# DoRA forward on Trainium2: hand-made semaphores in one critical section, and TensorE's blocks as a loop inside one instruction page

## The chip, the cores and the metric

The kernel runs on one core of a Trainium2 chip. The metric is the device time in microseconds (us) of one execution, the median of ten. Beside it stands one profiled execution: its span runs from the first to the last instruction of the program, and a little more time lies around it.

## The reference

```python
W_adapted = W + scale * (lora_A @ lora_B)
W_norm = np.sqrt(np.sum(W_adapted ** 2, axis=0, keepdims=True) + 1e-8)
W_final = W_adapted / W_norm * m
y = x.reshape(-1, 256) @ W_final          # x: 16 x 2048 x 256, float32
```

W is 256 x 256, the rank is 16. x and y are 33.5 MB each, so 67.1 MB cross between HBM and the on-chip memory.

## The kernel before

The 32,768 rows of x are cut into 8 blocks of 4,096 rows (`BLK`), 4 MB each; a partition holds 32 rows of a block. Five buffers hold x blocks (`XBUFS = 5`), and y is written over x in the same buffer. A block is worked in 8 chunks of 4 rows per partition (`CH`, 64 chunks in all, `NCH`).

Setup: three small loads are issued by ScalarE (lora_A, lora_B, m), W by SyncE, and then SyncE issues the loads of blocks 0 to 4. Meanwhile the engines compute `w_final` (bfloat16) from W, lora_A, lora_B and m in a chain that alternates between TensorE, VectorE (DVE) and ScalarE (ACT); its last step is the multiplication of line 132.

Each chunk goes through four engines. GpSimd (POOL) rounds x to bfloat16 (`xb`, L148). TensorE transposes it in four instructions, two bfloat16 values read as one float32 (`xt_ps`, L151). DVE copies the result to on-chip memory (`xt`, L155). TensorE multiplies it with `w_final` in 8 matmuls (`y_ps`, L166). ACT copies y into the x buffer (L174). TensorE's order is written out by hand: the transposes of chunk g+1 stand before the multiplies of chunk g, but at the end of a block the multiplies come first. Everything on TensorE is unrolled: 64 chunks one after the other.

After the last chunk of a block SyncE issues its store (L178), and, from block 1 on, the load of block b+4 into the buffer of block b-1 (L62), which waits until the store of block b-1 has landed. All loads and stores of x and y go through SyncE's queue (q1), the three small loads through ACT's (q10). Semaphores and waits are placed by the tile framework. In the profile the queues of kind "instruction" (q8 and q14) carry the engines' own program.

Of the kernel before, what the change touches and what calls it, by code (L numbers as in the profile page):

```python
# [10 lines left out]
@with_exitstack  # L11
def kernel(
    ctx: ExitStack,
    tc: tile.TileContext,
    x: bass.AP,
    W: bass.AP,
    lora_A: bass.AP,
    lora_B: bass.AP,
    m: bass.AP,
    scale: float,  # L20
    out: bass.AP,
):
    nc = tc.nc
    P = 128
    FP32 = mybir.dt.float32
    BF16 = mybir.dt.bfloat16
    AF = mybir.ActivationFunctionType
    ALU = mybir.AluOpType

    x_flat = x.flatten_outer_dims()  # L30
    out_flat = out.flatten_outer_dims()
    N, IN = x_flat.shape
    OUT = W.shape[1]
    R = lora_A.shape[1]
    KC = IN // P
    J = 4
    DJ = 32
    BLK = DJ * P
    NBLK = N // BLK

    assert IN == OUT and IN % P == 0 and OUT % P == 0 and N % BLK == 0

    XBUFS = 5
    CH = DJ // J
    NCH = NBLK * CH

    consts = ctx.enter_context(tc.tile_pool(name="consts", bufs=1))
    startup = ctx.enter_context(tc.tile_pool(name="startup", bufs=1))
    xpool = ctx.enter_context(tc.tile_pool(name="xpool", bufs=XBUFS))
    xbpool = ctx.enter_context(tc.tile_pool(name="xbpool", bufs=3))  # L50
    xtpool = ctx.enter_context(tc.tile_pool(name="xtpool", bufs=3))
    pp_xt = ctx.enter_context(tc.tile_pool(name="pp_xt", bufs=4, space=bass.MemoryType.PSUM))
    pp_y = ctx.enter_context(tc.tile_pool(name="pp_y", bufs=2, space=bass.MemoryType.PSUM))


    ctx.enter_context(tc.manual_schedule())

    x_tiles = {}

    def load_x(b):  # L60
        t = xpool.tile([P, DJ, IN], FP32, name="x_sb", tag="x_sb")
        nc.sync.dma_start(  # L62
            out=t,
            in_=x_flat[b * BLK : (b + 1) * BLK].rearrange("(p j) k -> p j k", p=P),
        )
        x_tiles[b] = t


    a_nat = startup.tile([P, KC, R], FP32)
    nc.scalar.dma_start(out=a_nat, in_=lora_A.rearrange("(p t) r -> p t r", t=KC))  # L70
    w_nat = startup.tile([P, KC, OUT], FP32)
    nc.sync.dma_start(out=w_nat, in_=W.rearrange("(p t) o -> p t o", t=KC))
    b_nat = startup.tile([R, OUT], FP32)
    nc.scalar.dma_start(out=b_nat, in_=lora_B)
    m_row = startup.tile([1, OUT], FP32)
    nc.scalar.dma_start(out=m_row, in_=m[None, :])
    for b in range(XBUFS):
        load_x(b)

    identity = consts.tile([P, P], FP32)  # L80
    make_identity(nc, identity)
    ones = consts.tile([P, P], FP32)
    nc.vector.memset(ones, 1.0)
    eps_col = startup.tile([P, 1], FP32)
    nc.vector.memset(eps_col, 1e-8)

    warm = startup.tile([P, 1], FP32)
    nc.scalar.activation(out=warm, in_=eps_col, func=AF.Sqrt)  # L88


    w_final = consts.tile([P, KC, OUT], BF16)

    b_bf = startup.tile([R, OUT], BF16)
    nc.vector.tensor_copy(out=b_bf, in_=b_nat)  # L94

    aT_ps = pp_y.tile([R, KC * P], FP32, tag="psy", name="aT_ps")
    for t in range(KC):
        nc.tensor.transpose(aT_ps[:, t * P : (t + 1) * P], a_nat[:, t, :], identity)  # L98
    aT = startup.tile([R, KC * P], BF16)
    nc.vector.tensor_copy(out=aT, in_=aT_ps)  # L100

    ab_ps = pp_y.tile([P, KC, OUT], FP32, tag="psy", name="ab_ps")
    for t in range(KC):
        nc.tensor.matmul(  # L104
            ab_ps[:, t, :], aT[:, t * P : (t + 1) * P], b_bf, start=True, stop=True
        )

    wa = startup.tile([P, KC, OUT], FP32)
    nc.vector.scalar_tensor_tensor(  # L109
        out=wa, in0=ab_ps, scalar=float(scale), in1=w_nat, op0=ALU.mult, op1=ALU.add  # L110
    )
    sq = startup.tile([P, KC, OUT], FP32)
    nc.vector.tensor_mul(out=sq, in0=wa, in1=wa)  # L113


    n2_ps = pp_y.tile([P, OUT], FP32, tag="psy", name="n2_ps")
    for t in range(KC):
        nc.tensor.matmul(n2_ps, ones, sq[:, t, :], start=(t == 0), stop=(t == KC - 1))  # L118
    norm = startup.tile([P, OUT], FP32)
    nc.scalar.activation(out=norm, in_=n2_ps, func=AF.Sqrt, bias=eps_col)  # L120

    mb_ps = pp_y.tile([P, OUT], FP32, tag="psy", name="mb_ps")
    nc.tensor.matmul(mb_ps, ones[0:1, :], m_row, start=True, stop=True)  # L123
    m_all = startup.tile([P, OUT], FP32)
    nc.vector.tensor_copy(out=m_all, in_=mb_ps)  # L125
    wam = startup.tile([P, KC, OUT], FP32)
    for t in range(KC):
        nc.vector.tensor_mul(out=wam[:, t], in0=wa[:, t], in1=m_all)  # L128
    rnorm = startup.tile([P, OUT], FP32)
    nc.vector.reciprocal(out=rnorm, in_=norm)  # L130
    for t in range(KC):
        nc.vector.tensor_mul(out=w_final[:, t], in0=wam[:, t], in1=rnorm)  # L132

    j_order = []
    for a in range(J // 2):
        j_order.append(a)
        j_order.append(a + J // 2)


    xts = {}  # L140

    def transposed(g):
        b, c = divmod(g, CH)
        rows = x_tiles[b][:, c * J : (c + 1) * J, :]


        xb = xbpool.tile([P, J, IN], BF16, name="xb")
        nc.gpsimd.tensor_copy(out=xb, in_=rows)  # L148
        xt_ps = pp_xt.tile([P, J * P], FP32, tag="psxt", name="xt_ps")
        for j in range(J):  # L150
            nc.tensor.transpose(  # L151
                xt_ps[:, j * P : (j + 1) * P], xb[:, j, :].bitcast(FP32), identity
            )
        xt = xtpool.tile([P, J * P, KC], BF16, name="xt")
        nc.vector.tensor_copy(  # L155
            out=xt.rearrange("p r t -> p (r t)").bitcast(FP32), in_=xt_ps
        )
        xts[g] = xt

    def multiplied(g):  # L160
        b, c = divmod(g, CH)
        xt = xts.pop(g)
        y_ps = pp_y.tile([P, J, OUT], FP32, tag="psy", name="y_ps")
        for t in range(KC):
            for j in j_order:
                nc.tensor.matmul(  # L166
                    y_ps[:, j, :],
                    xt[:, j * P : (j + 1) * P, t],
                    w_final[:, t, :],
                    start=(t == 0 and (j % (J // 2)) == 0),  # L170
                    stop=(t == KC - 1 and (j % (J // 2)) == (J // 2) - 1),
                )

        nc.scalar.copy(out=x_tiles[b][:, c * J : (c + 1) * J, :], in_=y_ps)  # L174


        if c == CH - 1:
            nc.sync.dma_start(  # L178
                out=out_flat[b * BLK : (b + 1) * BLK].rearrange("(p j) k -> p j k", p=P),
                in_=x_tiles[b],  # L180
            )
            if b >= 1 and b - 1 + XBUFS < NBLK:
                load_x(b - 1 + XBUFS)

    transposed(0)
    for g in range(NCH):


        first = (g + 1) % CH == 0
        if first:  # L190
            multiplied(g)
        if g + 1 < NCH:
            transposed(g + 1)
        if not first:
            multiplied(g)


# [33 lines left out]
```

## Time and profile before

| what | value |
|---|---|
| median of ten runs | 165.51 us (165.28 to 165.94) |
| the profiled execution, its own time | 165.39 us |
| its span | 163.5 us |
| bytes read from and written to HBM | 33.85 and 33.55 MB, 412 GB/s over the span |
| share of the span of q1, the queue of x and y | 96.6% of 16 DMA engines |
| ACT, POOL busy | 66.4 us, 66.5 us |
| TensorE matmul busy | 100.8 us |
| median from issue to landing: load of x, store of y | 29.3 us, 34.0 us |

The page cuts the span into 40 slices and gives for each the busy share in tenths. The chain of waits follows the work that ended last back to its beginning. In the queue table, the columns are packets, MB and share of 16 engines' span. In tables by stretch of time each row has the length of the stretch, the busy time (and count) of PE, its weight loads, DVE, ACT and POOL, TensorE's granted clock, the DMA share and GB/s. Single packets of the DMA queues, with start, length and size, are in the trace as well; times are counted from the span's start. A load or store of one block is 128 packets of 32,768 bytes, 8 on each of the 16 DMA engines, and leaves one packet of 4 bytes on each engine when that engine's share is done.

These waits of SyncE's queue show when SyncE stands still (us in total, times, longest):

```profile
SPq L178 <- ACT x_sb L174: 63.7, 5, 17.6
SPq L62 <- DMA out_dram<-x_sb: 49.1, 3, 22.1
SPq L226 <- DMA out_dram<-x_sb: 23.2, 1, 23.2
```

### The profile page before, as it was taken

To read this page: it belongs to the slowest core of one execution; us is meant where nothing else is said; L and a number is where in the kernel's file an instruction comes from. 1 tells how busy PE (TensorE), PEld (TensorE's weight loads), DVE (VectorE), ACT (ScalarE), POOL (GpSimd) and SP (SyncE) were. 2 spreads that over 40 slices of the span, in tenths; PEclk is the share of its full clock that TensorE was granted. 3 is DMA by queue.
4 is the path that set the end of the run, shared out by engine and by line. 5 is a ranking of instruction groups with operands and counts; after the bars stand their busy time and mean duration, and the time that the engine had idled before them with its cause. 6 is when DMAs were issued, how large, how long until landed. Compare 5 with 4: busy or idle time off the path is not lost.

```text
span 163.5 us, 2035 instructions
## 1 busy us (share of the span) xinstructions
PE 100.8 (62%) x778; PEld 84.9 (52%) x778; DVE 50.5 (31%) x76; ACT 66.4 (41%) x67; POOL 66.5 (41%) x70
## 2 busy tenths in 40 slices
PE   0264799999999999992009993299704997000000
PEld 0042589798898797991007891289603895000000
DVE  0228535455453654450003450055301352000000
ACT  3010147677678677674000675027800378000000
POOL 1005757687685886810029510595007750000000
PEclk9999999999999999999555899579995799955555
DMA  5998998999999999999999999999999999999981
GB/s 196 461 441 385 497 401 385 485 409 425 457 397 369 401 477 399 425 449 405 465 417 417 457 425 409 465 409 437 441 417 425 457 417 421 433 433 441 433 385 56
DMA packets 2635, 67.53 MB, mean 413 GB/s; under 512 B 433, under 2 KB 450, under 8 KB 578
## 3 DMA queue, kind: packets, MB, share of 16 engines
q1 hardware_dynamic: 2448, 67.37, 96.6%
q8 instruction: 6, 0.10, 0.2%
q10 hardware_dynamic: 178, 0.03, 0.1%
q14 instruction: 3, 0.02, 0.0%
HBM read 33.85 MB, written 33.55 MB: 412 GB/s over the span
## 4 chain that ended last, share of the span: by engine, by line
DMA 59%; PE 17%; DVE 4%; ACT 2%; issue 1%; POOL 1%; ACTq 0%; SPq 0%; POOLq 0%
DMA out_dram<-x_sb 38%; DMA x_sb<-in_x_dram 18%; PE y_ps L166 9%; PE xt_ps L151 5%; DMA b_nat<-in_lora_B_dram 3%; ACT x_sb L174 2%; PE n_ps L118 1%; DVE w_final L132 1%; DVE rnorm L130 1%; PE mb_ps L123 1%; POOL xb L148 1%; DVE wam L128 0%; DVE sq L113 0%; DVE wa L109 0%; PE ab_ps L104 0%
## 5 line engine op out<-in xcount | busy, mean ns | idle before, releaser
L148 POOL CAST xb<-x_sb 128x1024 bf16<-128x1024 f32 x64 | 65.8, 1046 | 66.1 <-DMA x_sb<-in_x_dram 47.1
L174 ACT COPY x_sb<-y_ps 128x1024 f32<-128x1024 f32 x64 | 64.4, 1013 | 62.4 <-PE y_ps L166 37.8
L166 PE MATMUL y_ps<-w_final,xt 128*128 128x256 bf16 x512 | 70.7, 286 | 2.3 <-DVE xt L155 2.3
L155 DVE COPY xt<-xt_ps 128x512 f32<-128x512 f32 x64 | 43.8, 691 | 75.6 <-PE xt_ps L151 75.6
L151 PE MATMUL xt_ps<-identity,xb 128*128 128x128 f32 x256 | 43.0, 301 | 26.4 <-POOL xb L148 26.4
L166 PEld LDWEIGHTS <-xt 128*128 128x128 bf16 x512 | 51.1, 102 | 12.7 <-DVE xt L155 5.8
L151 PEld LDWEIGHTS xt_ps<-identity,xb 128*128 128x128 f32 x256 | 33.4, 156 | 29.9 <-POOL xb L148 29.0
L120 ACT ACTIVATE norm<-n_ps,eps_col 128x256 f32<-128x256 f32 x1 | 0.5, 474 | 7.8 <-PE n_ps L118 7.8
L118 PE MATMUL n_ps<-sq,ones 128*128 128x256 f32 x4 | 2.0, 667 | 1.6 <-DVE sq L113 1.6
L98 PE MATMUL aT_ps<-identity,a_nat 128*16 128x128 f32 x2 | 0.6, 396 | 3.8 <-DMA a_nat<-in_lora_A_dram 3.8
L104 PE MATMUL ab_ps<-b_bf,aT 16*128 16x256 bf16 x2 | 0.6, 402 | 2.9 <-DVE aT L100 2.9
L118 PEld LDWEIGHTS n_ps<-sq,ones 128*128 128x128 f32 x4 | 1.2, 324 | 2.2 <-issue 2.0
L88 ACT ACT_TABLE_LOAD x1 | 1.3, 1283 | 2.2 <-issue 2.2
L98 PEld LDWEIGHTS aT_ps<-identity,a_nat 128*16 128x16 f32 x2 | 0.1, 88 | 3.8 <-issue 3.8
L94 DVE CAST b_bf<-b_nat 16x256 bf16<-16x256 f32 x1 | 0.3, 281 | 5.6 <-DMA b_nat<-in_lora_B_dram 5.6
L104 PEld LDWEIGHTS <-aT 16*128 16x128 bf16 x2 | 0.1, 102 | 3.4 <-DVE aT L100 3.4
L132 DVE TENSOR_TENSOR w_final<-wam,rnorm 128x256 bf16<-128x256 f32 x2 | 1.8, 920 | 0.0
L130 DVE RECIPROCAL rnorm<-norm 128x256 f32<-128x256 f32 x1 | 1.7, 1748 | 0.0
L125 DVE COPY m_all<-mb_ps 128x256 f32<-128x256 f32 x1 | 0.4, 425 | 3.4 <-PE mb_ps L123 3.4
L123 PE MATMUL mb_ps<-m_row,ones 1*128 1x256 f32 x2 | 1.2, 710 | 0.0
L109 DVE SCALAR_TENSOR_TENSOR wa<-ab_ps,w_nat 128x512 f32<-128x512 f32 x1 | 0.7, 691 | 0.7 <-PE ab_ps L104 0.7
L123 PEld LDWEIGHTS mb_ps<-m_row,ones 1*128 1x128 f32 x2 | 0.5, 308 | 0.7 <-issue 0.7
(12 smaller groups left out, 3.2 us busy)
## 6 DMA issues: line engine op xcount, KB each, us to landing
x_sb<-in_x_dram SPq DMA_DIRECT2D x8, 4096.0 KB, 29.3
out_dram<-x_sb SPq DMA_DIRECT2D x8, 4096.0 KB, 34.0
w_nat<-in_W_dram SPq DMA_DIRECT2D x1, 256.0 KB, 2.8
a_nat<-in_lora_A_dram ACTq DMA_DIRECT2D x1, 16.0 KB, 2.9
b_nat<-in_lora_B_dram ACTq DMA_DIRECT2D x1, 16.0 KB, 5.4
m_row<-in_m_dram ACTq DMA_DIRECT2D x1, 1.0 KB
```

Source lines behind the costliest of these rows:

```text
L88: nc.scalar.activation(out=warm, in_=eps_col, func=AF.Sqrt)
L98: nc.tensor.transpose(aT_ps[:, t * P : (t + 1) * P], a_nat[:, t, :], identity)
L104: nc.tensor.matmul(ab_ps[:, t, :], aT[:, t * P : (t + 1) * P], b_bf, start=True, stop=True)
L118: nc.tensor.matmul(n2_ps, ones, sq[:, t, :], start=(t == 0), stop=(t == KC - 1))
L123: nc.tensor.matmul(mb_ps, ones[0:1, :], m_row, start=True, stop=True)
L130: nc.vector.reciprocal(out=rnorm, in_=norm)
L132: nc.vector.tensor_mul(out=w_final[:, t], in0=wam[:, t], in1=rnorm)
L148: nc.gpsimd.tensor_copy(out=xb, in_=rows)
L151: nc.tensor.transpose(xt_ps[:, j * P : (j + 1) * P], xb[:, j, :].bitcast(FP32), identity)
L155: nc.vector.tensor_copy(out=xt.rearrange("p r t -> p (r t)").bitcast(FP32), in_=xt_ps)
L166: nc.tensor.matmul(y_ps[:, j, :], xt[:, j * P : (j + 1) * P, t], w_final[:, t, :], start=(t == 0 and (j % (J // 2)) == 0), stop=(t == KC - ...
L174: nc.scalar.copy(out=x_tiles[b][:, c * J : (c + 1) * J, :], in_=y_ps)
```

## The change

The tile framework's pools and automatic semaphores go. The whole kernel is one critical section (`tc.tile_critical()`), with buffers and semaphores made by hand, and each engine's program is written separately, one engine after the other. What is left out of the diff is the setup, written in the same manner.

```diff
-    ctx.enter_context(tc.manual_schedule())
+    NXB = 4
+    NXT = 4
+    ctx.enter_context(tc.tile_critical())
...
+    x_bufs = [sb(f"x_sb{k}", [P, DJ, IN], FP32) for k in range(XBUFS)]
+    xb_bufs = [sb(f"xb{k}", [P, J, IN], BF16) for k in range(NXB)]
+    xt_bufs = [sb(f"xt{k}", [P, F4, KC], BF16) for k in range(NXT)]
...
+    for b in range(NBLK):
+        nc.sync.wait_ge(sem("done"), b + 1)
+        nc.sync.dma_start(out=rows(out_flat, b), in_=x_bufs[b % XBUFS][:]).then_inc(
+            sem(f"store{b}"), 16
+        )
+        if b >= 1 and b - 1 + XBUFS < NBLK:
+            nc.sync.wait_ge(sem(f"store{b - 1}"), 16)
+            load_x(b - 1 + XBUFS)
+    for b in range(NBLK - XBUFS, NBLK):
+        nc.sync.wait_ge(sem(f"store{b}"), 16)
...
+        if g >= NXB:
+            nc.gpsimd.wait_ge(sem("turned"), g - NXB + 1)
+        nc.gpsimd.tensor_copy(
+            out=xb_bufs[g % NXB][:],
+            in_=x_bufs[b % XBUFS][:, c * J : (c + 1) * J, :],
+        ).then_inc(sem("rounded"), 1)
...
+        if c == CH - 1:
+            nc.scalar.drain().then_inc(sem("done"), 1)
...
+    nc.tensor.wait_ge(dv, 8)
+    nc.tensor.sem_inc(sem("room"), 2)
+
+    def take(name):
+
+        nc.tensor.sem_inc(sem(name), -1).wait_op(sem(name), 1, "sem-ge")
...
+    def turned(c):
+        take("rounded")
...
+        i.then_inc(sem("turned"), 1)
+
+    def product(c):
+        take("copied")
+        take("room")
...
+        i.then_inc(sem("product"), 1)
+
+    with nc.Fori(0, NBLK, 1, engines=[PE], head_slot={PE: 0}):
+        turned(0)
+        for c in range(CH):
+            if c + 1 < CH:
+                turned(c + 1)
+            product(c)
```

TensorE's 8 blocks are now one loop body that is run 8 times (`Fori` on TensorE alone); `head_slot` puts its first instruction at the beginning of an instruction page, with padding ahead of it that is jumped over. The waits inside the loop can't count upwards from pass to pass, so `take` waits until a semaphore is at least 1 and takes 1 off it. `wait_ge(dv, 8)` stands before the loop: no transpose of x is begun until `w_final` is done. The rounded and transposed chunks have 4 buffers each instead of 3. The setup's arithmetic, the number and size of the DMAs and the order of SyncE's queue are the same; the small intermediate products of the setup lie in the buffers of `y_ps`. The critical section begins with a NoOp of SyncE whose semaphore every engine waits for, and ends with an exchange of semaphores between SyncE and the other engines ahead of the closing barrier, which was there before. In the built program DVE, POOL and ACT have 89, 97 and 90 instructions instead of 146, 147 and 145, because most waits are now part of the instruction that waits.

## The prediction

> **What bounds the kernel now.** I read the page first, then the waits of SyncE's queue, then the end of the span in short stretches, then the single DMA packets.
>
> ```profile
> span 163.5 us, 2035 instructions
> PE 100.8 (62%) x778; PEld 84.9 (52%) x778; DVE 50.5 (31%) x76; ACT 66.4 (41%) x67; POOL 66.5 (41%) x70
> ...
> DMA  5998998999999999999999999999999999999981
> ...
> q1 hardware_dynamic: 2448, 67.37, 96.6%
> q8 instruction: 6, 0.10, 0.2%
> ...
> q14 instruction: 3, 0.02, 0.0%
> ...
> DMA 59%; PE 17%; DVE 4%; ACT 2%; issue 1%; POOL 1%; ACTq 0%; SPq 0%; POOLq 0%
> ```
>
> No compute engine is busy above 62%, while the DMA row is at 9 from the third slice to the last but two: the kernel is as long as 67.1 MB of x and y take on the 16 DMA engines. In the packet records each 32,768-byte packet takes 1.213 us and follows the one before on its engine at 1.210 us; 128 of them per engine are 154.9 us. The rest of the 163.53 us is the head (first x packets at 2.95 us), disturbances, and the tail. So I ask of each edit whether it changes one of those three, not what TensorE does.
>
> That TensorE has room is read from the last block:
>
> ```profile
> 136.92 1.97 ACT L174 COPY x_sb<-y_ps 128x1024 f32<-128x1024 f32 x2 [0.30 <-PE y_ps L166]
> 138.92 0.33 SPq L178 DMA_DIRECT2D out_dram<-x_sb  x1
> ```
>
> The last store is issued at 138.92. The store before it finishes between 149.14 and 152.40 on the 16 engines (each transfer leaves one 4-byte completion packet per engine, and these are the marks I use). The last store therefore waits 10.2 us in a full queue even on the earliest engine; the first, issued at 31.55, stands behind loads that end at 52.3.
>
> Now the tail, and the fetches of instructions:
>
> ```profile
> 158.00:158.80 0.80, 0.00 (x0) 0.00 (x0) 0.00 (x0) 0.00 (x0) 0.00 (x0) 0.50 0.95 410
> 158.80:159.60 0.80, 0.00 (x0) 0.00 (x0) 0.00 (x0) 0.00 (x0) 0.00 (x0) 0.50 0.38 164
> 159.60:160.40 0.80, 0.00 (x0) 0.00 (x0) 0.00 (x0) 0.00 (x0) 0.00 (x0) 0.50 0.38 164
> 160.40:161.20 0.80, 0.00 (x0) 0.00 (x0) 0.00 (x0) 0.00 (x0) 0.00 (x0) 0.50 0.19 82
> ```
>
> The last but one number is the DMA share, counted by the starts of packets: from 158.8 us on, fewer and fewer engines still have work. The last store's marks run from 158.82 to 162.08, mean 160.12. Equal packets were dealt to all 16, so the end is set by the one engine that was disturbed most, 3.26 us behind the best. What disturbed it shows in this stretch (30.0 to 31.2 us):
>
> ```profile
> q1 hardware_dynamic: 14, 0.46, 92.3%
> q8 instruction: 1, 0.02, 5.3%
> ```
>
> One 16,384-byte instruction packet at 30.07 took 1.026 us, and the data packet behind it, at 31.085, 1.762 instead of 1.213. Of the marks of the third load (22.58 to 23.12) and the fourth (32.31 to 32.85), all keep their places but one: it went from 0.22 behind the first to 1.75, so the fetch cost its engine 1.53 us. The second fetch (46.91; next packet 1.764) does the same to another engine. Just before the first store all engines meet slow packets (1.36 to 2.09 us, between 49.3 and 51.3); the two late engines meet the two longest, 2.63 and 2.75 us, and stand 2.40 and 2.68 behind after it. By the end they are, as far as the marks can be followed, the last two, 3.09 and 3.26 behind. The four later fetches (62.2, 75.6, 112.0, 136.1) hit other engines, at most 2.46 behind at the end.
>
> **The change, part by part.**
>
> *Fetches by TensorE.* Before, 1565 TensorE instructions make six fetches, about one in 260. After, some 40 setup instructions (with a branch into the loop), then a body of 217 run eight times (64 for 32 transposes as load and multiply, 128 for 64 matmuls, 23 semaphore instructions, 2 for the loop), all inside one page that begins at the loop head. Going round costs no fetch if a jump back inside a page fetches nothing. Entering that page is still a crossing, and in the trace every crossing has one fetch: 216, 504, 772, 985, 1272 and 1536 TensorE instructions are on record when the six start. So I count one fetch, at about 17.5 us, when w_final is done (15.61 + 1.76 = 17.37). It lies in the load-only stage like the fetch at 30.07, so it costs 1.53 us and its engine meets the slow packets late. That engine alone ends 3.1 to 3.26 behind: the maximum over 16 engines falls by 0 to 0.17 us although five of six fetches are gone. I take -0.1. With no fetch at all the last engine would be one of those that were never hit or hit late: bound -1.6 (to a lag of about 1.6, which the marks at the middle of the list, 0.56 to 1.60, suggest). With a fetch for each pass the bound is 0 to +0.6.
>
> [...]
>
> *Fetches by the others.* Three 8,192-byte packets at 57.4 (twice) and 63.3 come when DVE, POOL and ACT have 70 or so instructions on record. The new programs are shorter (89, 97 and 90 instead of 146, 147 and 145, separate waits folded away) but still pass 70, now in block 6, about 105 to 118 us. Three remain: 0, or +0.5 if one hits the last engine.
>
> *TensorE's pace.* The transposes of chunk 0 now stand behind w_final, not beside it (before: 15.00); three semaphore instructions per chunk stand in the queue, and the multiplies wait on two of them. From the 27 instructions per chunk instead of 24, and 1.31 us per chunk now, I take 1.5 us, so 12 to 13 us per block instead of 11.1, and 2 us lost at the entry. Behind a waiting TensorE stand DVE, ScalarE and the stores; the cover is the 10.2 us above for the last block (whose load sets its start), about 19 us for the first. Cost: 0. Were the cover gone, each us of TensorE would be one of the end: at over 2.6 us per chunk (1.31 + 10.2 / 8).
>
> *Head.* The critical section adds on SyncE, ahead of its first DMA, a NoOp and a branch that waits on its semaphore. SyncE's closing instructions follow each other at 0.06 us (162.463, 162.522, 162.583, ...), a semaphore needs 0.04 (614 to 656 ns at the start barrier). So 2 x 0.06 + 0.04 + some for the branch = +0.18 (0.1 to 0.35). All x data shift by this. The fifth load loses its wait for the small a load (it went at 3.69): nothing, 16 MB lie ahead of it.
>
> *Tail.* From the last mark (162.08) to SyncE's wake-up 0.38, from there to its barrier 0.37 in six steps, then 0.70. After: ten steps (event, two branches, event, drain, two events, NoOp, branch, drain) and in them one exchange with four engines: 10 x 0.06 + 0.15 = 0.75, so +0.38 (0.2 to 0.6).
>
> ScalarE's drain ahead of each store and the extra xb and xt buffers lie inside the cover: 0.
>
> **Sum.** Against the profiled run: 163.53 + 0.18 - 0.10 + 0.38 = 163.99, and 1.86 around it (165.39 - 163.53): 165.85. That run is 0.12 below the median of 165.51, so on the median's scale 165.97; since the branch terms are roundings upward, I say 165.9.
>
> **Rivals.**
>
> A, one fetch at the entry, as above: 165.9, own range 165.5 to 166.4. Chance 0.62.
>
> B, no fetch in the stream, or one on an engine that leads: the page behind is there already, or nothing asks for it. For it: the body never leaves its page, and TensorE's first two pages were there without a fetch in the span. Against: six crossings, six fetches. The last engine comes 1.2 to 1.6 us sooner, head and tail stay: 165.51 + 0.56 - 1.4 = 164.7 (164.4 to 165.0). It is the side other than my forecast, and decides if no 16,384-byte packet lies between 10 and 49 us. Chance 0.23.
>
> C, the jump back fetches anew each pass: eight fetches, three of them before 49 us, none on the way of compute by the cover. If one engine takes two: +0.56 + 0.6 = 166.6; else as A. I say 166.4. For it: a jump is not a fall-through, and no row shows one. Chance 0.11.
>
> D, TensorE loses its cover: a stall of some us at each wait or jump. It would have to double the pace; nothing among the waits is that long. At 3.0 us per chunk, 0.4 x 8 = 3.2 us: 169. Chance 0.04.
>
> **Numbers.** Time 165.9 (A). Range 164.5 to 166.5: all of A, most of B and C, about two in ten outside. A change under 0.2% (0.33 us) can't be told from none here. A gives slower 0.35, same 0.25, faster 0.02; B faster 0.23; C and D slower 0.14, same 0.01. Faster 0.25, same 0.26, slower 0.49.
>
> **What would show it.** Right: one q8 packet in the span, near 17.5 us, the packet behind it about 1.76 us long; fifteen marks of the last store within about 2.2 us and one alone at some 3 us; first x data near 3.1; 1.8 us from last mark to end. Wrong: no q8 packet before 49 us (B), eight (C), a DMA share under 0.9 between 30 and 158 us (D), or head and tail grown by over 1 us.

## The result and the profile after

The changed kernel takes 166.34 us (median of 9 runs, 166.14 to 166.41). The kernel before, run beside it, takes 165.55 us (median of 32 runs, 165.26 to 166.18). The ratio, formed from all runs and not from the two medians, is 1.0041 with an interval of 1.0030 to 1.0052: slower by 0.3 to 0.5%, about 0.7 us. The forecast of 165.9 us lay on the right side and its range holds the time; of the size it gave somewhat over half (0.39 us over its base of 165.51).

The first lines of the page of the changed kernel, its queue table and its chain of waits:

```profile
span 164.4 us, 2075 instructions
...
PE 100.4 (61%) x778; PEld 84.4 (51%) x778; DVE 51.2 (31%) x76; ACT 66.8 (41%) x67; POOL 66.2 (40%) x70
...
DMA  5998999989999998999999999999999999999970
...
q1 hardware_dynamic: 2448, 67.37, 96.0%
...
q8 instruction: 1, 0.02, 0.0%
q14 instruction: 3, 0.02, 0.0%
...
PE 1%; ACT 1%; issue 0%
```

The compute engines are as busy as before, and the DMA row is at 8 or 9 from the third slice to the last but two, as before. q8 went from 6 packets to 1: the loop does what it says. q1 moved the same bytes, and its share fell only because the span grew from 163.5 to 164.4 us. The chain is short here because it could be followed back only over the last product and copy; it says nothing of what lies ahead of them, so SyncE's waits and the packets have to do.

SyncE's waits in the changed kernel (us in total, times, longest):

```profile
SPq L123 <- ACTq L205: 83.2, 5, 28.6
SPq L104 <- DMA out_dram<-x_sb: 48.4, 3, 21.2
SPq L130 <- DMA out_dram<-x_sb: 23.0, 2, 13.4
SPq L303 <- PEq L303: 0.8, 2, 0.6
SPq L289 <- PEq L289: 0.7, 1, 0.7
```

Two more rows of this view of the kernel before:

```profile
SPq L178 <- DMA x_sb<-in_x_dram: 17.5, 3, 9.8
SPq L226 <- PEq L226: 0.6, 2, 0.4
```

The waits ahead of a store name ScalarE's drain (L205) in place of its copy. Before, the same stops were booked in two rows, 63.7 us to the copy and 17.5 us to landing loads, 81.2 together; the 83.2 us now are 2.0 more, and they lie ahead of stores that then stand in a full queue (9.9 us even for the last one, below). The waits for landed stores (L104, L130) are within 0.7 us of those before. So nothing in the stops between the first store and the last explains the loss; behind the last store the closing barrier's wait grew, to 0.8 us from 0.6. What is left is before the first packet, after the last, and in the stream itself.

The end of the stream in the changed kernel, in the same stretches as before:

```profile
158.00:158.80 0.80, 0.00 (x0) 0.00 (x0) 0.00 (x0) 0.00 (x0) 0.00 (x0) 0.50 1.23 532
158.80:159.60 0.80, 0.00 (x0) 0.00 (x0) 0.00 (x0) 0.00 (x0) 0.00 (x0) 0.50 0.29 123
159.60:160.40 0.80, 0.00 (x0) 0.00 (x0) 0.00 (x0) 0.00 (x0) 0.00 (x0) 0.50 0.10 41
160.40:161.20 0.80, 0.00 (x0) 0.00 (x0) 0.00 (x0) 0.00 (x0) 0.00 (x0) 0.50 0.10 41
161.20:162.00 0.80, 0.00 (x0) 0.00 (x0) 0.00 (x0) 0.00 (x0) 0.00 (x0) 0.50 0.10 41
```

The last but one number is again the DMA share by starts of packets. Most engines now stop together: 13 of the 16 marks lie before 159.9 us, against 9 before (a share of 0.10 is about one packet in 0.8 us; before, 0.38 went on to 160.4). A share over 1 comes from counting a packet where it starts. But the last one stops no sooner. In the marks of the last store, the mean engine is 0.78 us behind the first, against 1.30 before; the last is 3.45 behind, against 3.26. Five fetches fewer made the average engine earlier and the end no earlier.

From these two profiled executions the 0.87 us of the span can be booked in full:

| | before | after | difference |
|---|---|---|---|
| SyncE issues its first DMA | 0.74 | 0.94 | +0.21 |
| earliest mark of the first load | 12.86 | 12.89 | +0.03 |
| earliest mark of the last store | 158.82 | 159.09 | +0.27 |
| last mark of the last store | 162.08 | 162.54 | +0.46 |
| from there to the end of the span | 1.44 | 1.86 | +0.41 |

### The profile page after: what moved, and what is told of

It reads as the page before. It is cut to its first block, busy times and chain, and to the rows that moved or that the text cites. A ratio compares the mean times of both kernels' runs of the same rounds, so it can differ in the third digit from the quotient of the medians.

```text
span 164.4 us, 2075 instructions
## 1 busy us (share of the span) xinstructions
PE 100.4 (61%) x778; PEld 84.4 (51%) x778; DVE 51.2 (31%) x76; ACT 66.8 (41%) x67; POOL 66.2 (40%) x70
## 5 line engine op out<-in xcount | busy, mean ns | idle before, releaser
L246 PE MATMUL xt_ps<-identity,xb 128*128 128x128 f32 x256 | 42.0, 297 | 27.4 <-PEq L235 27.4
L258 PEld LDWEIGHTS y_ps<-w_final,xt 128*128 128x128 bf16 x512 | 50.9, 102 | 14.9 <-issue 8.3
L223 PE MATMUL y_ps<-sq,ones 128*128 128x256 f32 x4 | 2.1, 671 | 1.6 <-DVE sq L169 1.6
L194 ACT ACTIVATE norm<-y_ps,eps_col 128x256 f32<-128x256 f32 x1 | 0.5, 474 | 6.1 <-PE y_ps L223 6.1
L212 PE MATMUL y_ps<-identity,a_nat 128*16 128x128 f32 x2 | 0.6, 396 | 3.5 <-DMA a_nat<-in_lora_A_dram 3.5
L223 PEld LDWEIGHTS y_ps<-sq,ones 128*128 128x128 f32 x4 | 1.2, 322 | 2.3 <-DVE sq L169 2.1
L216 PE MATMUL y_ps<-b_bf,aT 16*128 16x256 bf16 x2 | 0.6, 402 | 1.5 <-DVE aT L162 1.5
L228 PE MATMUL y_ps<-m_row,ones 1*128 1x256 f32 x2 | 1.2, 710 | 0.0
L165 DVE SCALAR_TENSOR_TENSOR wa<-y_ps,w_nat 128x512 f32<-128x512 f32 x1 | 0.7, 692 | 0.8 <-PE y_ps L216 0.8
L228 PEld LDWEIGHTS y_ps<-m_row,ones 1*128 1x128 f32 x2 | 0.5, 306 | 0.7 <-issue 0.7
```

Of the source, the lines that this page charges most:

```text
L165: nc.vector.scalar_tensor_tensor(out=wa[:], in0=ab_ps, scalar=float(scale), in1=w_nat[:], op0=ALU.mult, op1=ALU.add).then_inc(dv, 1)
L212: i = nc.tensor.transpose(aT_ps[:, t * P : (t + 1) * P], a_nat[:, t, :], identity[:])
L223: i = nc.tensor.matmul(n2_ps, ones[:], sq[:, t, :], start=(t == 0), stop=(t == KC - 1))
L228: nc.tensor.matmul(mb_ps, ones[0:1, :], m_row[:], start=True, stop=True).then_inc(pe, 1)
L246: i = nc.tensor.transpose(xt_ps[c % 4][:, j * P : (j + 1) * P], xb_bufs[c % NXB][:, j, :].bitcast(FP32), identity[:],)
L258: i = nc.tensor.matmul(y_ps[c % 2][:, j, :], xt_bufs[c % NXT][:, j * P : (j + 1) * P, t], w_final[:, t, :], start=(t == 0 and (j % (J // 2 ...
```

## The experiments

Each ratio is against runs of the kernel before on the same chip. "Marks" are the 4-byte completion packets again.

**Loop, page and fetch inside the section.** Three kernels keep the section and change TensorE's program alone.

```diff
 e1_unrolled
-    with nc.Fori(0, NBLK, 1, engines=[PE], head_slot={PE: 0}):
+    for _ in range(NBLK):
 e2_half_first_page: half a block per pass, not aligned
+    with nc.Fori(0, 2 * NBLK, 1, engines=[PE]):
+        for c in range(4):
 e3_half_own_page: as e2, aligned
+    with nc.Fori(0, 2 * NBLK, 1, engines=[PE], head_slot={PE: 0}):
```

> The changed kernel with TensorE's eight blocks written out again, all else kept. Theory (the end is set by the one DMA engine that an early instruction fetch delays; head and closing part cost 0.4 to 0.5 us more): six fetches come back, two of them before 49 us, on two engines; the last engine ends 3.1 to 3.5 us behind the first, as with the loop; 166.1 to 166.5 us, ratio to before 1.003 to 1.006. Rival 'the loop, its jumps and its takes cost the time': back to 165.5 to 165.8. Rival 'each fetch adds to the end': 166.8 or more.

> The loop body is half a block (4 chunks, 16 passes, 109 instructions) and is not aligned, so that setup and loop lie in TensorE's first page. Theory: no 16,384-byte packet in the span; no engine alone 3 us behind, the next one (2.6 in the changed kernel) sets the end; about 0.9 us sooner than the changed kernel, 165.2 to 165.7. Rival 'fetches do not matter, head and tail are all': 166.2 to 166.5. Rival 'a jump back fetches': 16 fetches, 166.3 or more.

> As the half-block loop, but aligned to the head of the second page, the only difference. Theory: one fetch some 3 us after the loop is entered, one engine 3.1 to 3.5 us behind, 166.1 to 166.5. Rivals as for the half-block loop in the first page: the same time as that one.

| kernel | fetches (q8) | median, us | ratio, interval | last three marks behind the first |
|---|---|---|---|---|
| e1, unrolled | 6 | 166.25 | 1.0045, 1.0027 to 1.0064 | 2.26, 2.53, 3.85 |
| e2, half, first page | 0 | 166.55 | 1.0060, 1.0042 to 1.0078 | 0.99, 1.19, 3.64 |
| e3, half, own page | 1 | 166.12 | 1.0042, 1.0026 to 1.0058 | 0.63, 3.00, 3.30 |

Six fetches, none or one: all three lose what the change loses. The loop is neither the cost nor a gain. e2 is the case of no fetch that rival B needed: by B's price it was to be 1.4 us faster, by its own forecast 0.9, and it was neither. Its queue table, and then its end in stretches:

```profile
q1 hardware_dynamic: 2448, 67.37, 95.6%
q10 hardware_dynamic: 178, 0.03, 0.1%
q14 instruction: 3, 0.02, 0.0%
```

```profile
159.60:160.40 0.80, 0.00 (x0) 0.00 (x0) 0.00 (x0) 0.00 (x0) 0.00 (x0) 0.50 0.10 41
160.40:161.20 0.80, 0.00 (x0) 0.00 (x0) 0.00 (x0) 0.00 (x0) 0.00 (x0) 0.50 0.00 0
161.20:162.00 0.80, 0.00 (x0) 0.00 (x0) 0.00 (x0) 0.00 (x0) 0.00 (x0) 0.50 0.09 41
```

There is no q8 row at all, fifteen engines are done within 1.19 us of the first, and still one engine starts a packet between 161.2 and 162.0 us. It had met no fetch of TensorE. From the first store on, the place of the latest mark behind the earliest went 0.57, 1.12, 1.64, 1.84, 2.80, 2.99, 3.00, 3.30, 3.63, 3.64, 3.64: a little is lost in most transfers while the compute engines run (from 130.8 to 138.4 us this engine's packets take 1.26 to 1.28 us, not 1.213), nearly 1 us in one load (a packet of 2.19 us at 100.4), and nothing once the compute engines stand still, after 141 us.

**The loop across a page.** The body is left where it falls, behind the setup. That it crosses from the first page into the second in each of its 8 passes is an estimate, and a close one: some 40 setup instructions and a body of 217, against six fetches for 1565 TensorE instructions, about one in 260, in the kernel before. The trace does not show where a page begins.

```diff
-    with nc.Fori(0, NBLK, 1, engines=[PE], head_slot={PE: 0}):
+    with nc.Fori(0, NBLK, 1, engines=[PE]):
```

> The changed kernel without the alignment of the loop head: the body of 217 instructions begins behind the setup in the first page and ends in the second. Theory: each pass crosses into the second page, so 8 fetches if a crossing always fetches, 1 if the page ahead is still there; the jump back may stall TensorE, the cover hides it. Time by the worst engine: 166.1 to 166.8 us, ratio 1.003 to 1.008. Rival 'the alignment inside a page is what this loop lives by': over 167.5.

The ratio is 1.0058, 1.0039 to 1.0078, from 4 runs: no different from the change. The queue table of its page has one fetch for the whole span; the second fence is the same table for the stretch from 43 to 44.5 us:

```profile
q8 instruction: 1, 0.02, 0.0%
```

```profile
q1 hardware_dynamic: 19, 0.62, 96.2%
q8 instruction: 1, 0.02, 4.5%
```

One fetch (at 43.46 us, 1.07 us long) for eight passes: coming back to the loop's head fetched nothing more. The fetch came in the third pass, so neither of the first two passes made one; what set it off there is not known. The alignment by `head_slot` bought nothing here. No run here jumped back further than over a body of 217 instructions.

**More semaphores.** A term that I had not foreseen: in the trace, GpSimd clears the range of semaphores between the two closing barriers (one EVENT_SEMAPHORE_RANGE_CLEAR, at 163.14 us before and at 163.86 after), in 96 ns before (12 semaphores) and 243 ns after (37). Forty more, used for nothing:

```diff
+    for k in range(40):
+        sem(f"spare{k}")
```

> The changed kernel with 40 more semaphores allocated and never used. Theory: the closing clear goes through a range of 77 instead of 37 and grows from 0.243 to about 0.48 us (12 took 0.096 before, so 5.9 ns each); 166.55 to 166.6 us. Rival 'the length of the clear has nothing to do with their number': 166.3.

The clear took 460 ns for 77 semaphores, and the time from the last mark to the end 2.13 us instead of 1.86. With 203 ns for 31 and 163 for 24 in the kernels below, that is some 5.6 ns for each semaphore (364 ns more for the 65 from 12 to 77). The time is 1.0064, 1.0039 to 1.0089; it overlaps the change's own interval, so the clear itself is shown, and its 0.13% in the time only agrees.

**Without the section.** e6 keeps every engine's program, the loop and its alignment, and takes away the critical section and the frame around it; e7 does so with the half loop of e2 and 24 semaphores, which it gets by using the load and store semaphores of blocks 0 to 2 again for blocks 5 to 7 and one semaphore of GpSimd's for two purposes.

```diff
-    ctx.enter_context(tc.tile_critical())
...
-            sems[name] = tc.alloc_semaphore(name)
+            sems[name] = nc.alloc_semaphore(name)
...
+    nc.all_engine_barrier()
+    nc.clear_and_free_semaphores(list(sems.values()))
+    nc.all_engine_barrier()
```

> The changed kernel without the critical section and the tile framework around it: same engine programs, loop and fetch; at the end one barrier, the clear of the semaphores (31 instead of 37) and one barrier. Theory (head and closing part of the section cost): SyncE's first DMA at 0.74 instead of 0.94 us, last mark to end 1.85 to about 1.55; 0.4 to 0.5 us below the changed kernel, ratio to before 1.001 to 1.003. Rival 'the hand-made semaphores and the loop cost the time': ratio stays at 1.004. Rival 'the fetch alone costs it': the same, 1.004.

> As the kernel without the section, with the half-block loop in the first page (no fetch by TensorE) and 24 semaphores instead of 31. Theory as it stands now (without a fetch the engine that creeps behind during the stores ends last, 2.5 to 3.6 us behind): 0.04 us less in the clear, and 0 to 0.6 us less by the lag; ratio to before 0.997 to 1.002. Rival 'an early fetch is what sets the end': ratio 0.993 to 0.996.

e6 is 0.9994, 0.9984 to 1.0004; e7 is 1.0001, 0.9989 to 1.0014. Neither can be told from the kernel before, and both are clear of the change's 1.0030. e6 differs from the change in nothing but the section, its frame and six semaphores, so the loss sits there, and not in the hand-made semaphores, the extra buffers or ScalarE's drains, which e6 keeps: 1.0041 against 0.9994 is 0.78 us. It gave back more than the 0.4 to 0.5 us that was expected. From e6's page and then its waits of SyncE:

```profile
span 163.5 us, 2059 instructions
...
q8 instruction: 1, 0.02, 0.0%
```

```profile
SPq L122 <- ACTq L204: 84.2, 6, 28.3
...
SPq L292 <- PEq L292: 0.7, 1, 0.7
SPq L275 <- PEq L275: 0.6, 1, 0.6
SPq L273 <- PEq L273: 0.2, 1, 0.2
```

The same single fetch, the same waits for ScalarE, and a span of 163.5 us. Its last two rows are the two closing barriers. From the last mark to the end it takes 1.26 us, 0.59 less than the change, and SyncE issues its first DMA at 0.74 us, 0.20 earlier; the two make 0.79 of the 0.78 us. e7, with no fetch, again has one engine 3.73 us behind: the second witness against rival B.

**The head by itself.** e9 holds SyncE's first DMA back in e6, behind a wait for GpSimd; e10 lets every engine wait at the entry for a signal of SyncE, as the section does, but without its branch.

```diff
 e9_late_start
+    nc.sync.wait_ge(sem("pool"), 1)
     nc.sync.dma_start(
 e10_all_wait_at_entry
+    nc.sync.sem_inc(sem("go"), 1)
+    for e in (nc.sync, nc.scalar, nc.vector, nc.gpsimd, nc.tensor):
+        e.wait_ge(sem("go"), 1)
```

> The kernel without the section, but SyncE's first DMA waits for GpSimd's first memset, some 0.2 us, as long as the section's entry held it. Theory A (the entry's 0.2 us are passed on to the end, and a later start also changes what all engines lose at the first store): first DMA near 0.95 us, loss at the first store 0.9 to 1.1 instead of 0.68, 165.47 + 0.1 + 0.3 = 165.8 to 166.0. Theory B (the loss at the first store has another cause): loss 0.6 to 0.7, 165.5 to 165.7.

> The kernel without the section, but every engine first waits for a semaphore that SyncE sends, as in the section's entry; only the branch is missing. Theory A: first DMA near 0.85 us, 165.6 to 165.9, with a loss at the first store between 0.7 and 1.1. Theory B: 165.5 to 165.6, loss 0.6 to 0.7.

In e9 the first DMA came at 0.96 us, as late as in the change, and the time is 1.0015, 1.0002 to 1.0027, so about 0.35 us over e6, with an uncertainty of some 0.25: a late start of 0.22 us costs something, and about what it is late by is within that. The loss at the first store was 0.74 us, not the 0.9 to 1.1 of theory A. In e10 it came at 0.80 and the time is 0.9999, 0.9987 to 1.0011: a wait of all engines costs nothing that can be seen. There the loss at the first store was 1.00 us without a loss of time that can be seen, so neither theory holds whole.

**The head made shorter.** In e6 and in the kernel before, W's load is issued by ScalarE, behind lora_A and lora_B and ahead of m, so that SyncE begins with x.

```diff
-    nc.sync.dma_start(out=w_nat[:], ...)
...
     nc.scalar.dma_start(out=b_nat[:], ...)
+    nc.scalar.dma_start(out=w_nat[:], ...)
     nc.scalar.dma_start(out=m_row[:], ...)
```

> The kernel without the section, with the load of W moved from SyncE to ScalarE's queue (behind lora_A and lora_B), so that x is SyncE's first DMA. Theory (the end is the DMA stream, which starts with the first x packet): x packets from 2.5 instead of 2.9 us, W lands late between them and w_final some us later, which the cover hides; 0.3 to 0.45 us below 165.47, ratio to before 0.996 to 0.998. Rival 'later weights hold up the compute': 165.5 or more.

> The same move of W's load in the kernel before, nothing else changed. Theory: as there, 0.3 to 0.45 us, ratio 0.9973 to 0.998. Rival: 1.000 or more.

Both missed: e11 is 1.0060, 1.0041 to 1.0078 (6 runs), e12 is 1.0017, 0.9997 to 1.0037. x did start sooner (first load's earliest mark at 12.10 and 12.17 us, not 12.8), but W did not arrive. The DMA issues (KB each, us from issue to landing) of the changed kernel, and then of e11:

```profile
w_nat<-in_W_dram SPq DMA_DIRECT2D x1, 256.0 KB, 2.8
a_nat<-in_lora_A_dram ACTq DMA_DIRECT2D x1, 16.0 KB, 2.5
b_nat<-in_lora_B_dram ACTq DMA_DIRECT2D x1, 16.0 KB, 3.6
```

```profile
w_nat<-in_W_dram ACTq DMA_DIRECT2D x1, 256.0 KB, 24.6
a_nat<-in_lora_A_dram ACTq DMA_DIRECT2D x1, 16.0 KB, 12.6
b_nat<-in_lora_B_dram ACTq DMA_DIRECT2D x1, 16.0 KB, 14.6
```

256 KB took 24.6 us instead of 2.8. The packets tell why: each engine's 8 packets of lora_A (13 ns each) come at 1.22 us from each other, its 8 packets of W (84 ns each) at 1.30 us, from 15.8 to 24.5 us. Between any two of them there is room for one 32 KB packet of x (1.213 us), beside the 128 bytes of a packet of lora_A as beside the 2 KB of one of W. In e12's chain of waits (start, us, what) W is the longest early piece:

```profile
1.65 24.51 DMA w_nat<-in_W_dram
```

w_final is late by some 17.5 us, and the first store with it: issued at 49.52 us in e11 and 48.06 in e12, instead of 31.86 (e6) and 31.55 (before). In e11's waits of SyncE:

```profile
SPq L122 <- ACTq L204: 120.3, 8, 46.2
...
SPq L103 <- DMA out_dram<-x_sb: 13.8, 3, 10.5
```

The waits for compute grew from e6's 84.2 us to 120.3 and those for landed stores shrank from 48.8 to 13.8: compute now runs just ahead of the queue. e11's second store is issued at 61.07 us, 0.4 us before the first one lands on its earliest engine, and the next two transfers take 10.66 and 11.03 us by these marks instead of 9.68: the cover of the stores is used up. The 0.7 us gained at the head were gone before that, in e12 as in e11. The 8 packets of W take the same 0.67 us of each engine, only later, and by the third load's earliest mark (32.29 us in e11, 32.22 in e6; 32.34 in e12, 32.31 before) nothing is left of the lead.

**The kernel before once more.** e5 is the unchanged kernel, for the spread of a profile.

> The kernel before once more, for a second profile of it. Theory: again 1.44 us from the last completion mark to the end, first x packets near 2.95 us. Open: whether the loss of all engines at the first store (0.62 us in the first profile of before, 0.89 to 1.16 in five profiles with the critical section) and the lag of the last engine (3.26) were this kernel's or chance.

One run, 165.68 us. Its tail (1.45 us) and clear (96 ns) repeat those of before to 0.01, its loss at the first store is 0.68 us (0.62) and its last engine 3.46 us behind (3.26); its last mark, 162.35, is 0.27 later. So the end of the stream is known from one profile only to 0.2 or 0.3. A tail is known better: the change, e1, e3 and e8 agree on 1.85 within 0.01, though e2 has 1.98 (the 0.13 us more lie ahead of SyncE's wake-up).

## Why the prediction was right in its mechanism and short in its size

**One fetch, on entry: right.** One q8 packet in the span, at 20.43 us. The queue table of the changed kernel from 20 to 22 us:

```profile
q1 hardware_dynamic: 31, 1.02, 119.1%
q8 instruction: 1, 0.02, 3.1%
```

The fetch took 0.99 us and the data packet behind it 1.71, so its engine went to 1.75 us behind. It then met the longest packet before the first store (3.18 us, at 51.05), stood 2.84 behind after it and 3.45 at the end, close to the forecast (3.1 to 3.26), with fourteen of the others within 1.45 us and one at 2.57. The fetch came 3.4 us after the loop had begun (17.03 us), not at the jump, and TensorE's matmuls are busy for the whole 0.99 us beside it (20.43 to 21.42 us): no fetch in the span brought the instructions that the loop began with. The three q14 fetches came at 66.2, 97.6 and 106.1 us, not all between 105 and 118. Followed packet by packet, each set its engine back by 0.4 to 0.7 us; none of the three is the last, so the end does not show it. (What the prediction calls the third and the fourth load in its reading of the first fetch are the second and the third load of x; it counts W's there.)

**No fetch per pass: rival C falls.** Eight passes, one fetch, in the change and also in e8.

**TensorE keeps its cover: rival D falls, and my pace was too slow.** The timeline of TensorE's matmuls around the first jump back, in the changed kernel:

```profile
26.45 1.04 PE L258 MATMUL y_ps<-w_final,xt 128*128 128x256 bf16 x8
27.32 0.60 PE L246 MATMUL xt_ps<-identity,xb 128*128 128x128 f32 x4
27.76 1.04 PE L258 MATMUL y_ps<-w_final,xt 128*128 128x256 bf16 x8
28.63 0.60 PE L246 MATMUL xt_ps<-identity,xb 128*128 128x128 f32 x4
29.07 1.04 PE L258 MATMUL y_ps<-w_final,xt 128*128 128x256 bf16 x8
30.26 1.03 PE L258 MATMUL y_ps<-w_final,xt 128*128 128x256 bf16 x8 [0.15 <-PEq L235]
31.13 1.04 PE L246 MATMUL xt_ps<-identity,xb 128*128 128x128 f32 x8
32.76 1.03 PE L258 MATMUL y_ps<-w_final,xt 128*128 128x256 bf16 x8 [0.59 <-PEq L235]
```

A chunk takes 1.31 us (26.45 to 27.76, 27.76 to 29.07), as before: three semaphore instructions per chunk cost nothing, where I had taken 0.2 us. The jump back lies ahead of the transposes at 31.13, and they start with no idle time shown. The waits of 0.15 and 0.59 us around them are not the jump's: unrolled, e1 has the same two at the same places. A block takes 11.55 us from the first store to the second (32.40 to 43.95), not 12 to 13 (before: 11.09; e1: 11.60). The first store is issued 0.85 us later than before, not 2; among the whole-block kernels with the section it is issued anywhere from 29.76 us (e1) to 32.40, so this part is not measured by one profile. The end of the last block:

```profile
137.37 1.03 PE L258 MATMUL y_ps<-w_final,xt 128*128 128x256 bf16 x8 [0.15 <-PEq L235]
138.44 1.01 ACT L201 COPY x_sb<-y_ps 128x1024 f32<-128x1024 f32 x1 [0.17 <-PE y_ps L258]
139.51 0.33 SPq L123 DMA_DIRECT2D out_dram<-x_sb  x1
```

The last store is issued at 139.51 and the one before it lands on its earliest engine at 149.41: 9.9 us of cover, against 10.2 before.

**Tail: right (+0.38 forecast, +0.41 measured), for a part by luck.** From SyncE's wake-up to its barrier the change takes 0.63 us against 0.37, so the exchange costs +0.26, less than I had counted. The rest is the longer clear, +0.15, which I did not see: I had read SyncE's rows up to the barrier and left the 0.70 behind it as a constant.

**The term that came out too small: head and last engine, +0.08 together in the sum, +0.46 in the pair of profiles.** The parts went otherwise than forecast.

SyncE's delay was right (+0.18 forecast, +0.21 measured), though the first load's earliest mark came only 0.03 later in this pair (12.90 against 12.80 as means over six kernels with the section and five without that start at the usual time).

The lag, forecast 0.1 smaller, came out 0.19 larger, inside what two profiles of one kernel differ by.

And a loss appeared that I had no term for: at the end of the fifth load, just ahead of the first store, where all engines meet slow packets, even the earliest engine loses 0.96 us instead of 0.62. In six profiles with the section this loss is 0.89 to 1.16; in five without it 0.58 to 0.74, but in e10, also without it, 1.00. So the section is not shown to be its cause, and what sets it stays open; nor is it passed on to the end in full, for e10's last mark is only 0.11 us behind e6's.

Over six profiles with the section and six without, the last mark lies at 162.63 and 162.37 in the mean: +0.26 with a standard error of 0.13 (one of the six without, e9, starts as late as those with). With +0.41 of tail that makes 0.67, the 0.7 us of the ratio. The forecast was short by 0.3 us (0.39 against 0.68): 0.07 of it is its last step from 165.97 down to 165.9, 0.03 the tail, and 0.18 this stream, which is little more than its standard error.

That the fetched engine is the last one came true, but by luck as far as the time goes: with no fetch at all (e2, e7) the last engine stands as far behind, so no run supports the term of -0.1 that was taken from it.

**Rival B was priced wrongly, and would have misled had it come true.** It took "the fetched engine is the last" to mean "without the fetch the end comes 1.2 to 1.6 us sooner". e2 and e7 have no fetch and end with one engine 3.64 and 3.73 us behind. What comes next in line I had read from the middle of the list of marks; it was another engine, of another cause, as late as the first. It could have been seen: followed packet by packet, the kernel before has an engine that meets no fetch and still ends 2.46 us behind, next after the two fetched ones, and the change has one at 2.57. Why that one engine is slow was not tried, and why it falls back further in the two kernels without a fetch is open too.

No version beat the kernel before by what can be measured; e6 and e10, the best, are within 0.2% of it.

## What to carry to other kernels

In a kernel that is as long as its transfers, an edit to a covered engine's program (a loop, fewer instructions, fewer fetches) was worth nothing here (e1, e2 and e3: 1.0042 to 1.0060, the change 1.0041); look at what it puts ahead of the first packet and behind the last. Entering and leaving a critical section (0.21 us more ahead of the first DMA, 0.26 of exchange behind the last mark), and each semaphore that has to be cleared at the end (some 5.6 ns), lie there here; read all rows of the tail, not only those that an edit touches. Where the end is the latest of 16 engines, taking away what delayed that one did not give back its lag here (3.64 and 3.73 us in e2 and e7 without a fetch, 3.45 in the change with one): find out first who is next and why.

## What the runs showed of the hardware that I had not expected

- A loop of 217 TensorE instructions, run 8 times and not aligned to a page, fetched once (e8, at 43.46 us). Beside the changed kernel's one fetch TensorE's matmuls were busy for all of its 0.99 us (20.43 to 21.42).
- The clear of the semaphores' range at the end takes 96, 163, 203, 243 and 460 ns for 12, 24, 31, 37 and 77 semaphores (the kernel before, e7, e6, the change, e4).
- One DMA engine's packets take 1.25 to 1.30 us instead of 1.213 in stretches while compute engines run and stores are under way, in the kernel before (54.9 to 72.9 us, 125.6 to 138) as in the changed one (55.1 to 73.0, 129.7 to 137.4), and it ends 2.3 to 3.7 us behind, as far as packets can be followed by their times.
- A load of 256 KB on another engine's queue, behind a stream that fills the 16 DMA engines, took 24.6 us (e11) instead of 2.8: its packets of 2 KB (84 ns) came at 1.30 us from each other, one for about each 32 KB packet of the stream (1.213 us), and not as an equal share of the bytes.
